# HGRN2 heads of a two-layer hybrid: urgent level steps, z from PSUM, output times z before the root factor, a second gate tile and a 32-byte tile

## Chip, cores and metric

The kernel runs on one core of a Trainium2 chip. The metric is the device time of one execution in microseconds, as a median over runs. The core's engines each work through their own instructions in order: TensorE (PE, with its weight loads shown as PEld), VectorE (DVE), ScalarE (ACT), GpSimd (POOL) and SyncE (SP, which here only issues DMAs).

## The reference

A stream of 1024 latent tokens and 256 context tokens, 1024 wide, goes through two layers. Layer 0 has neighbourhood-attention and mLSTM heads, layer 1 has 16 HGRN2 heads, which the change concerns. The arithmetic is fp32. Of layer 1, cut to the core:

```python
q, f_fwd, f_bwd, i, z = split(h @ w_in)                  # 2048 columns each, 16 heads of 128
f = lb + (1 - lb) * sigmoid(f_pre)                        # per direction
rec = silu(q), i, ((1 - f, log f) forward, (1 - f, log f) backward)
# per head and direction, S starts from the context's final state:
#   S_t = diag(f_t) S_(t-1) + (1 - f_t) i_t^T ;   o_t = S_t^T silu(q_t)
o = o_forward + o_backward
y = (rms(o, h_norm) * silu(z)) @ w_out
x = x + gate * y
```

## The kernel before, in words

The kernel is written in a tile framework. The order in which the program issues operations gives each a priority; the framework's scheduler keeps, with modelled times, the order of each engine by those priorities and by what is ready, and the engines then follow that order. `filler` adds 1000000 to the priority number of what it encloses, so that it comes last among what is ready. Tiles belong to pools; a tile name with n buffers waits for the buffer used n allocations before. Pools open from the left end of the core's SBUF, or, with `side="right"`, from its right end. PSUM has two banks each of "mm" (projection sums) and "tr" (transposes); while the heads run, three of "s" and one of "acc".

The large fp32 products are written in three parts, each with the fp32r type: `dense` (L125 to L131) multiplies high part by high part (L128), and the two mixed ones (L129, L130). They are called products in the text. Layer 0 and its output projection take the first 1880 us, the HGRN2 heads 1880 to 3350 us, the last output projection the rest.

The heads go one after another (the loop over `h` in `build`). For each:

- `hg_proj` (L882) makes the gates F (two directions, 1024 tokens) and Fc (256 context tokens) and q of the head, by products with 256 or 512 columns. Its weight slabs come from pool "w1" at the right. F and Fc are single tiles in a pool of their own (`self.fp`).
- `hg_intra` (L968) makes K = 1 - F, Q = q F (L979), and 32 small matmuls, the "strips" (`strip`, L995 to L997), for the diagonal blocks; then seven `hg_level` calls (L1016). Level l combines neighbouring blocks of 2^l tokens: ACT copies the chosen half of K into ksel (L1024), 32 strips multiply it with the chosen half of Q into a PSUM bank, DVE merges the result into D (`copy_predicated`, L1042), multiplies the other halves of K and Q in place by the block totals T (L1050), and makes the totals of the doubled blocks in a new tile gT0 to gT6 (L1052). At level 0, T is F itself. Strips of a level need Q and ksel of the level before.
- `hg_vz` (L912) makes v and z, by products of 256 columns with weights wzh and wzl in pool "hg" at the left. Of z's PSUM bank ACT makes a sigmoid (L933) and a copy (L934), and POOL multiplies the two (L935).
- `hg_close` transposes K; `hg_ctx` makes the context states; `hg_scan` (L1055) runs the recurrence over eight chunks and makes the outputs, in two halves of four chunks. A half stands in the only "acc" bank (L1073 to L1075): ACT squares and sums it (L1089), POOL makes the root factor ss (L154, L156), and DVE multiplies output, ss and z for each chunk (L1093), into z's tile.
- `hg_out` (L1128) transposes that z on TensorE (L1133), ACT scales it and POOL issues its DMA. It comes after `hg_proj` of the next head.
- `wo_sums` (L1103) and `y_diff` (L1119) prepare the last projection on POOL: four loads, four subtractions and four stores per call, one call in heads 0 to 7, two in heads 8 to 11.

So TensorE's stream of a head mixes products, strips, scan matmuls and transposes, and what stands between two strip groups is set by the scheduler.

Of the kernel before, what the change touches and what calls it, by code (L numbers as in the profile page):

```python
# [9 lines left out]
F32 = mybir.dt.float32  # L10
# [3 lines left out]
ALU = mybir.AluOpType  # L14
# [4 lines left out]
P = 128  # L19
D = 1024  # L20
KD = D // P
LAT = 1024
CTX = 256
SQ = 256
T = LAT + CTX
# [19 lines left out]
class Prog:  # L45
# [285 lines left out]
    @contextmanager  # L331
    def filler(self):
        p = self.tc.cur_priority
        self.tc.cur_priority = p + 1000000
        yield
        self.tc.cur_priority = p

# [544 lines left out]
    def hg_proj(self, h, pool, w=None):  # L882
        nc, a = self.nc, self.a
        st = {}
        col = lambda i: a["wc"][:, i * 2048 + h * P : i * 2048 + (h + 1) * P]
        lb, olb = self.lb[:, 0, h : h + 1], self.lb[:, 1, h : h + 1]
        F = self.t(self.fp, [P, 2, LAT], F32, "gF", 1)
        Fc = self.t(self.fp, [P, 2, CTX], F32, "gFc", 1)
        todo = [(d, t0, n) for d in range(2) for t0, n in ((LAT, CTX), (512, 512), (0, 512))]
        if w:  # L890

            todo.sort(key=lambda x: x[1] == 0)
        w = w or [None, None]
        for d, t0, n in todo:
            w[d] = w[d] or self.wring([col(1 + d)], P)
            ps = self.ps("mm", [P, n])
            self.proj_tr(ps, w[d], 0, t0, n)
            dst = Fc[:, d, :] if t0 == LAT else F[:, d, t0 : t0 + 512]
            nc.scalar.activation(dst, ps, AF.Sigmoid)
            nc.vector.tensor_scalar(out=dst, in0=dst, scalar1=olb, scalar2=lb, op0=ALU.mult, op1=ALU.add)  # L900
        q = {}
        w = self.wring([col(0)], P)
        for t0 in (512, 0):
            ps = self.ps("mm", [P, 512])
            self.proj_tr(ps, w, 0, t0, 512)
            q[t0 // 512] = self.t(pool, [P, 512], F32, "gq", 2)
            sg = self.t(pool, [P, 512], F32, "gsg", 1)
            nc.scalar.activation(sg, ps, AF.Sigmoid)
            nc.vector.tensor_tensor(out=q[t0 // 512], in0=sg, in1=ps, op=ALU.mult)
        return dict(F=F, Fc=Fc, q=q)  # L910

    def hg_vz(self, h, st, pool):  # L912
        nc, a = self.nc, self.a
        col = lambda i: a["wc"][:, i * 2048 + h * P : i * 2048 + (h + 1) * P]
        w = self.wblock(pool, "wz", [col(3), col(4)], KD, 256)
        v = self.t(pool, [P, NT, P], F32, "gv", 2)
        z = self.t(pool, [P, NT - 2, P], F32, "gz", 1)
        ps = self.ps("mm", [P, CTX])
        self.proj_tr(ps, w, 0, LAT, CTX)
        vT = self.t(pool, [P, CTX], F32, "gEc", 1)  # L920
        nc.scalar.copy(vT, ps)
        pt = self.ps("tr", [P, 2, P])
        for j in range(2):
            nc.tensor.transpose(pt[:, j, :], vT[:, j * P : (j + 1) * P], self.ident)
        nc.scalar.copy(v[:, 8:10, :], pt)
        for tt in range(0, 8, 2):

            ps = self.ps("mm", [P, 2, 256])
            for j in range(2):
                self.proj_nat(ps[:, j, :], w, tt + j, 0, 256)  # L930
            nc.scalar.copy(v[:, tt : tt + 2, :], ps[:, :, 0:P])
            sg = self.t(pool, [P, 2, P], F32, "gsg", 1)
            nc.scalar.activation(sg, ps[:, :, P:256], AF.Sigmoid)  # L933
            nc.scalar.copy(z[:, tt : tt + 2, :], ps[:, :, P:256])  # L934
            nc.gpsimd.tensor_tensor(out=z[:, tt : tt + 2, :], in0=z[:, tt : tt + 2, :], in1=sg, op=ALU.mult)  # L935
        st["v"], st["z"] = v, z


# [29 lines left out]
    def hg_intra(self, st, pool):  # L968
        nc = self.nc
        F, q = st["F"], st["q"]  # L970
        K = self.t(pool, [P, 2, LAT], F32, "gK", 1)
        nc.vector.tensor_scalar(out=K, in0=F, scalar1=-1.0, scalar2=1.0, op0=ALU.mult, op1=ALU.add)
        Q = self.t(pool, [P, 2, LAT], F32, "gQ", 1)
        ks = [self.t(pool, [P, 512], F32, "gkn", 4) for _ in range(2)]
        for hf in (1, 0):
            s = slice(hf * 512, (hf + 1) * 512)
            nc.vector.tensor_tensor(out=ks[hf], in0=K[:, 0, s], in1=K[:, 1, s], op=ALU.add)
            for d in range(2):
                nc.vector.tensor_tensor(out=Q[:, 1 - d, s], in0=q[hf], in1=F[:, d, s], op=ALU.mult)  # L979
        hv = dict(Q=Q, K=K, T=F, D=self.t(pool, [P, 8, 64], F32, "gD", 1))  # L980
        hv["A"] = self.t(pool, [P, 8, P], F32, "gA", 1)
        pa = self.ps("s", [P, 8, 64])
        for c in range(8):
            for b in range(2):
                o = c % 4 * P + b * 64
                self.strip(pa[:, c, :], b, ks[c // 4][:, o : o + 64], q[c // 4][:, o : o + 64])
        nc.vector.tensor_tensor(
            out=hv["D"], in0=pa, in1=self.lmask[:, 0, :].unsqueeze(1).to_broadcast([P, 8, 64]), op=ALU.mult
        )
        for lev in range(7):  # L990
            self.hg_level(hv, lev, pool)
        return hv
# [23 lines left out]
    def hg_level(self, H, lev, pool):  # L1016
        nc = self.nc
        n, h = LAT, 1 << lev
        nb = n // (2 * h)
        K, Q, A, D, Tt = H["K"], H["Q"], H["A"], H["D"], H["T"]  # L1020

        pick = lambda t: _skew(t[:, 0, :].rearrange("p (b s i) -> p b s i", s=2, i=h), 2, n)
        ksel = self.t(pool, [P, n], F32, "gksel", 1)
        nc.scalar.copy(ksel.rearrange("p (b s i) -> p b s i", s=2, i=h), pick(K))  # L1024
        pa = self.ps("s", [P, 8, 64])
        for c in range(8):
            for b in range(2):
                o = c * P + b * 64
                out = pa[:, c, :]
                if lev < 6:  # L1030
                    out = out.rearrange("p (b s i) -> p b s i", s=2, i=h)
                    rhs = pick(Q)[:, o // (2 * h) : (o + 64) // (2 * h)]
                else:
                    rhs = Q[:, 1 - b, c * P + (1 - b) * 64 : c * P + (2 - b) * 64]
                self.strip(out, b, ksel[:, o : o + 64], rhs)
        for b in range(2):
            s, e = slice(b * 64, (b + 1) * 64), slice((1 - b) * 64, (2 - b) * 64)
            if lev == 6:
                nc.scalar.copy(A[s, :, s], D[s])
                nc.scalar.copy(A[s, :, e], pa[s])  # L1040
        if lev < 6:
            nc.vector.copy_predicated(D, self.lmask[:, lev + 1, :].unsqueeze(1).to_broadcast([P, 8, 64]), pa)  # L1042
        Tv = Tt.rearrange("p d (b s) -> p d b s", s=2)


        m = 2 * nb
        for t, o, step in ((K, 1, m - 1), (Q, m + 1, -m - 1)):
            v = bass.AP(t.tensor, t.offset, [list(t.ap[0]), [n + h, 2], [2 * h, nb], [1, h]])
            tot = bass.AP(Tt.tensor, Tt.offset + o, [list(Tt.ap[0]), [step, 2], [2, nb], [0, h]])
            nc.vector.tensor_tensor(out=v, in0=v, in1=tot, op=ALU.mult)  # L1050
        Tn = self.t(pool, [P, 2, nb], F32, f"gT{lev}", 1)
        nc.vector.tensor_tensor(out=Tn, in0=Tv[:, :, :, 0], in1=Tv[:, :, :, 1], op=ALU.mult)  # L1052
        H["T"] = Tn

    def hg_scan(self, st, H, S, pool):  # L1055
        nc = self.nc
        v, z = st["v"], st["z"]
        Sf, Sb = S
        sb = {7: Sb}
        for c in range(7, 0, -1):  # L1060
            u = self.ps("s", [P, P])
            nc.tensor.matmul(u, lhsT=H["kn"][c // 4][1][:, c % 4, :], rhs=v[:, c, :], start=True, stop=True)
            s = self.t(pool, [P, P], F32, "gS1", 10)
            nc.vector.scalar_tensor_tensor(
                out=s, in0=sb[c], scalar=H["T"][:, 1, c : c + 1], in1=u, op0=ALU.mult, op1=ALU.add
            )
            sb[c - 1] = s
        for c in range(8):
            cs = slice(c * P, (c + 1) * P)
            if c % 4 == 0:  # L1070
                o4 = self.ps("acc", [P, 4, P])
            o = o4[:, c % 4, :]
# [3 lines left out]
            if c < 7:  # L1076
                u = self.ps("s", [P, P])
                nc.tensor.matmul(u, lhsT=H["kn"][c // 4][0][:, c % 4, :], rhs=v[:, c, :], start=True, stop=True)
                s = self.t(pool, [P, P], F32, "gS0", 2)
                nc.vector.scalar_tensor_tensor(  # L1080
                    out=s, in0=Sf, scalar=H["T"][:, 0, c : c + 1], in1=u, op0=ALU.mult, op1=ALU.add
# [4 lines left out]
            ss = self.t(pool, [P, 4], F32, "gss", 2)  # L1086
# [2 lines left out]
                nc.scalar.activation(jk, o4[:, i, :], AF.Square, accum_out=ss[:, i : i + 1])  # L1089
            self.rsqrt(ss, ss, 1.0 / P)  # L1090

            for i in range(c - 3, c + 1):
                nc.vector.scalar_tensor_tensor(  # L1093
                    out=z[:, i, :], in0=o4[:, i % 4, :], scalar=ss[:, i % 4 : i % 4 + 1], in1=z[:, i, :],
                    op0=ALU.mult, op1=ALU.mult,
                )

    def quarters(self, pool):
        two = [self.t(pool, [P, 2 * SQ], F32, t, 1) for t in ("gknc", "gEc")]
# [39 lines left out]
    def build(self):  # L1139
        tc, nc, a = self.tc, self.nc, self.a  # L1140
        dma = nc.sync.dma_start
        with ExitStack() as es:
# [22 lines left out]
            def load(name, shape, eng=nc.gpsimd):  # L1165
# [12 lines left out]
                out=self.qkn, in0=qkn[:, 0:1], scalar1=qkn[:, 1:2], scalar2=0.125, op0=ALU.mult, op1=ALU.mult  # L1178
# [22 lines left out]
            )  # L1201


            right = ExitStack()
            es.enter_context(right)
            self.open_h(right)
# [397 lines left out]
```

## Time and profile before

| | us |
|---|---|
| median of 3 runs | 3482.99 |
| lowest and highest run | 3482.43, 3485.25 |
| profiled execution, its own time | 3489.74 |
| span of the profile | 3488.0 |
| granted TensorE clock (1 is full) | 0.993 |
| busy: PE, DVE, ACT, POOL | 3409.5, 2098.0, 1478.0, 707.3 |

The span is what the profile covers; the run's own time is 1.7 us longer. A row of the timeline shows start, duration, engine, line, operation, output tile <- input tiles, output shape, input shape, and how many alike instructions are taken together (x32); the bracket has the idle time before it and what ended that. `gz`, `gq`, `gK` and so on are the tiles of the code; a product's row, mm<-wzh,hh, has the stationary and moving operands in no fixed order.

### The profile page before, as it was taken

The numbers are of one execution on the slowest core, as the hardware profiler recorded it, in microseconds if no ns is written. First come the engines' busy times: TensorE is split into PE (matmuls) and PEld (weight loads), VectorE is DVE, ScalarE is ACT, GpSimd is POOL, SyncE is SP. The second block draws the span as 40 slices with busy tenths as digits, with TensorE's granted clock in tenths as the row PEclk, the third lists the DMA queues.
The fourth block names the chain that finished last, engine by engine and source line by source line (L and its number), as shares of the span: only waits on it lengthen the run. The fifth ranks groups of instructions, "written<-read, shape, count | busy, mean of one in ns | idle before, by whom it ended". The sixth has DMA issues, their size and how long they took to land.

```text
span 3488.0 us, 64893 instructions
## 1 busy us (share of the span) xinstructions
PE 3409.5 (98%) x25100; PEld 2990.6 (86%) x25100; DVE 2098.0 (60%) x4855; ACT 1478.0 (42%) x3433; POOL 707.3 (20%) x1076
## 2 busy tenths in 40 slices
PE   8999999999999999999999999999999999999997
PEld 5679998889989888898888988988888888888876
DVE  4546665666655566777666555555555555555667
ACT  5445554554543444454354333333333333333442
POOL 2222221222111112221100112222223222100023
PEclk9999999999999999999999999999999999999999
DMA  5542222322233434444752111111112111110274
GB/s 202 175 130 61 79 77 76 91 78 75 79 89 99 145 117 127 132 129 143 218 162 70 46 58 55 58 59 58 57 57 67 61 58 49 49 37 31 85 233 151
DMA packets 331540, 333.60 MB, mean 96 GB/s; under 512 B 30984, under 2 KB 277960, under 8 KB 331232
## 3 DMA queue, kind: packets, MB, share of 16 engines
q1 hardware_dynamic: 291008, 222.76, 22.0%
q0 software_dynamic: 40224, 106.69, 9.0%
q8 instruction: 198, 3.24, 0.4%
q14 instruction: 110, 0.90, 0.1%
HBM read 259.40 MB, written 69.79 MB: 94 GB/s over the span
## 4 chain that ended last, share of the span: by engine, by line
PE 85%; DMA 4%; issue 3%; DVE 3%; POOL 2%; ACT 1%; SPq 0%; POOLq 0%; DVEq 0%; ACTq 0%
PE mm L128 18%; PE mm L129 18%; PE mm L130 18%; PE s L997 4%; PE acc L775 2%; PE mm L837 2%; PE mm L835 2%; PE mm L836 2%; PE tr L755 2%; PE acc L547 2%; PE s L556 2%; PE acc L537 1%; PE tr L1009 1%; PE acc L1073 1%; PE acc L1074 1%
## 5 line engine op out<-in xcount | busy, mean ns | idle before, releaser
L128 PE MATMUL mm<-hh,wh 128*128 128x512 f32 (+1 forms) x1600 | 584.5, 365 | 0.0
L129 PE MATMUL mm<-hl,wh 128*128 128x512 f32 (+1 forms) x1600 | 584.3, 365 | 0.0
L130 PE MATMUL mm<-hh,wl 128*128 128x512 f32 (+1 forms) x1600 | 583.5, 365 | 0.0
L128 PE MATMUL mm<-wh,hh 128*128 128x256 f32 (+1 forms) x1520 | 471.2, 310 | 1.7 <-ACT ev L317 0.6
L129 PE MATMUL mm<-wl,hh 128*128 128x256 f32 (+1 forms) x1520 | 469.9, 309 | 0.0
L130 PE MATMUL mm<-wh,hl 128*128 128x256 f32 (+1 forms) x1520 | 468.9, 309 | 0.3 <-DVE hl L262 0.3
L130 PEld LDWEIGHTS mm<-hh,wl 128*128 128x128 f32 x1600 | 301.3, 188 | 45.6 <-issue 0.6
L129 PEld LDWEIGHTS mm<-hl,wh 128*128 128x128 f32 x1600 | 301.6, 188 | 43.8 <-issue 0.2
L128 PEld LDWEIGHTS mm<-hh,wh 128*128 128x128 f32 x1600 | 301.6, 188 | 43.0 <-issue 0.2
L128 PEld LDWEIGHTS mm<-wh,hh 128*128 128x128 f32 x1520 | 286.5, 189 | 16.5 <-issue 0.9
L129 PEld LDWEIGHTS mm<-wl,hh 128*128 128x128 f32 x1520 | 286.5, 188 | 14.7 <-issue 2.9
L130 PEld LDWEIGHTS mm<-wh,hl 128*128 128x128 f32 x1520 | 286.4, 188 | 13.8 <-issue 1.5
L128 PE MATMUL mm<-wzh,hh 128*128 128x256 f32 x1024 | 292.8, 286 | 0.6 <-ACT gz L934 0.6
L129 PE MATMUL mm<-wzl,hh 128*128 128x256 f32 x1024 | 292.8, 286 | 0.0
L130 PE MATMUL mm<-wzh,hl 128*128 128x256 f32 x1024 | 291.5, 285 | 0.0
L73 DVE TENSOR_TENSOR wl<-wraw,wh 128x512 fp32r<-128x512 f32 x240 | 165.5, 694 | 129.2 <-ACT wh L72 121.5
L72 ACT CAST wh<-wraw 128x512 fp32r<-128x512 f32 x240 | 147.2, 618 | 198.9 <-PE mm L129 140.7
L1024 ACT COPY gksel<-gK 128x1024 f32<-128x1024 f32 x112 | 128.0, 1143 | 213.0 <-PE s L997 139.2
L128 PEld LDWEIGHTS mm<-wzh,hh 128*128 128x128 f32 x1024 | 193.5, 189 | 3.8 <-ACT gz L934 1.6
L129 PEld LDWEIGHTS mm<-wzl,hh 128*128 128x128 f32 x1024 | 193.4, 189 | 1.0
L130 PEld LDWEIGHTS mm<-wzh,hl 128*128 128x128 f32 x1024 | 193.3, 189 | 1.0
L835 PE MATMUL mm<-woh,yh 128*128 128x512 f32 x422 | 170.4, 404 | 9.8 <-DVE og L1366 5.2
(390 smaller groups left out, 7623.4 us busy)
## 6 DMA issues: line engine op xcount, KB each, us to landing
wraw<-in_wab_dram SPq DMA_DIRECT2D x112, 256.0 KB
wraw<-in_wc_dram SPq DMA_DIRECT2D x96, 256.0 KB
wraw<-yd SPq DMA_DIRECT2D x94, 256.0 KB
adar<-in_wada_dram POOLq DMA_DIRECT2D x32, 512.0 KB, 4.5
wraw<-in_wc_dram SPq DMA_DIRECT2D x128, 128.0 KB
md<-ev POOLq DMA_DIRECT2D x60, 256.0 KB, 2.8
mloz<-md SPq DMA_DIRECT2D x40, 256.0 KB
adar<-in_wada_dram SPq DMA_DIRECT2D x16, 512.0 KB
```

Of the source, the lines that this page charges most:

```text
L72: nc.scalar.copy(hi, x)
L73: nc.vector.tensor_tensor(out=lo, in0=x, in1=hi.bitcast(F32), op=ALU.subtract)
L128: mm(ps, lhsT=lh(k), rhs=rh(k), start=(start and k == 0), stop=False)
L129: mm(ps, lhsT=lh(k), rhs=rl(k), start=False, stop=False)
L130: m = mm(ps, lhsT=ll(k), rhs=rh(k), start=False, stop=(stop and k == nk - 1))
L547: nc.tensor.matmul(num, lhsT=qc[:, j, :], rhs=C[d][:, j, :], start=False, stop=(j == 1))
L556: nc.tensor.matmul(u, lhsT=st["k"][c][:, j * P : (j + 1) * P], rhs=vw, start=True, stop=True)
L755: nc.tensor.transpose(pt[:nk, i, :], pr[:, o : o + nk], self.ident)
L775: m = nc.tensor.matmul(yp[h64], lhsT=v[:, h64], rhs=pTs[hd][:nk, i, :], start=(i == turn[0]), stop=(i == turn[-1]), tile_position=(0, hd * ...
L835: mm(ps, lhsT=yh[k], rhs=w.h(kk), start=(kk == 0), stop=False)
L997: self.nc.tensor.matmul(out[s], lhsT=lhsT, rhs=rhs, start=True, stop=True, tile_position=(0, b * 64))
L1024: nc.scalar.copy(ksel.rearrange("p (b s i) -> p b s i", s=2, i=h), pick(K))
```

## The change

It has six parts.

1. A new context, `urgent`, subtracts 1000000 from the priority number. It stands around the strips of the diagonal blocks, and in a level around the ksel copy, the strips, and the steps of Q, K and T. The merge into D is not in it.
2. T of the next level is written in place over T's own tile (F), level by level; only the last one goes to a tile of its own. The last level takes its stationary operand from K itself, with no ksel copy.
3. F and Fc of odd heads come from pool "hg", those of even heads from the pool they had.
4. z times its sigmoid is one DVE operation from PSUM; the copy on ACT and the product on POOL go.
5. A half of the outputs is multiplied by z on DVE in one operation over four chunks, without the root; POOL then multiplies it by the root factors, which are broadcast along 128 columns.
6. A tile of 32 bytes per partition is opened at the right end of SBUF ahead of everything else there, and zeroed once.

```diff
@@ -332,6 +332,14 @@
     def filler(self):
         p = self.tc.cur_priority
         self.tc.cur_priority = p + 1000000
+        yield
+        self.tc.cur_priority = p
+
+
+    @contextmanager
+    def urgent(self):
+        p = self.tc.cur_priority
+        self.tc.cur_priority = p - 1000000
         yield
         self.tc.cur_priority = p
 
@@ -884,8 +892,9 @@
         st = {}
         col = lambda i: a["wc"][:, i * 2048 + h * P : i * 2048 + (h + 1) * P]
         lb, olb = self.lb[:, 0, h : h + 1], self.lb[:, 1, h : h + 1]
-        F = self.t(self.fp, [P, 2, LAT], F32, "gF", 1)
-        Fc = self.t(self.fp, [P, 2, CTX], F32, "gFc", 1)
+        fp = pool if h % 2 else self.fp
+        F = self.t(fp, [P, 2, LAT], F32, "gF", 1)
+        Fc = self.t(fp, [P, 2, CTX], F32, "gFc", 1)
         todo = [(d, t0, n) for d in range(2) for t0, n in ((LAT, CTX), (512, 512), (0, 512))]
         if w:
 
@@ -931,8 +940,7 @@
             nc.scalar.copy(v[:, tt : tt + 2, :], ps[:, :, 0:P])
             sg = self.t(pool, [P, 2, P], F32, "gsg", 1)
             nc.scalar.activation(sg, ps[:, :, P:256], AF.Sigmoid)
-            nc.scalar.copy(z[:, tt : tt + 2, :], ps[:, :, P:256])
-            nc.gpsimd.tensor_tensor(out=z[:, tt : tt + 2, :], in0=z[:, tt : tt + 2, :], in1=sg, op=ALU.mult)
+            nc.vector.tensor_tensor(out=z[:, tt : tt + 2, :], in0=sg, in1=ps[:, :, P:256], op=ALU.mult)
         st["v"], st["z"] = v, z
 
 
@@ -980,10 +988,11 @@
         hv = dict(Q=Q, K=K, T=F, D=self.t(pool, [P, 8, 64], F32, "gD", 1))
         hv["A"] = self.t(pool, [P, 8, P], F32, "gA", 1)
         pa = self.ps("s", [P, 8, 64])
-        for c in range(8):
-            for b in range(2):
-                o = c % 4 * P + b * 64
-                self.strip(pa[:, c, :], b, ks[c // 4][:, o : o + 64], q[c // 4][:, o : o + 64])
+        with self.urgent():
+            for c in range(8):
+                for b in range(2):
+                    o = c % 4 * P + b * 64
+                    self.strip(pa[:, c, :], b, ks[c // 4][:, o : o + 64], q[c // 4][:, o : o + 64])
         nc.vector.tensor_tensor(
             out=hv["D"], in0=pa, in1=self.lmask[:, 0, :].unsqueeze(1).to_broadcast([P, 8, 64]), op=ALU.mult
         )
@@ -1020,37 +1029,37 @@
         K, Q, A, D, Tt = H["K"], H["Q"], H["A"], H["D"], H["T"]
 
         pick = lambda t: _skew(t[:, 0, :].rearrange("p (b s i) -> p b s i", s=2, i=h), 2, n)
-        ksel = self.t(pool, [P, n], F32, "gksel", 1)
-        nc.scalar.copy(ksel.rearrange("p (b s i) -> p b s i", s=2, i=h), pick(K))
-        pa = self.ps("s", [P, 8, 64])
-        for c in range(8):
-            for b in range(2):
-                o = c * P + b * 64
-                out = pa[:, c, :]
-                if lev < 6:
-                    out = out.rearrange("p (b s i) -> p b s i", s=2, i=h)
-                    rhs = pick(Q)[:, o // (2 * h) : (o + 64) // (2 * h)]
-                else:
-                    rhs = Q[:, 1 - b, c * P + (1 - b) * 64 : c * P + (2 - b) * 64]
-                self.strip(out, b, ksel[:, o : o + 64], rhs)
+        out = self.ps("s", [P, 8, 64])
+        with self.urgent():
+            if lev < 6:
+                ksel = self.t(pool, [P, n], F32, "gksel", 1)
+                nc.scalar.copy(ksel.rearrange("p (b s i) -> p b s i", s=2, i=h), pick(K))
+            for c in range(8):
+                for b in range(2):
+                    o = c * P + b * 64
+                    r = out[:, c, :]
+                    if lev < 6:
+                        r = r.rearrange("p (b s i) -> p b s i", s=2, i=h)
+                        lhsT, rhs = ksel[:, o : o + 64], pick(Q)[:, o // (2 * h) : (o + 64) // (2 * h)]
+                    else:
+                        lhsT = K[:, b, o : o + 64]
+                        rhs = Q[:, 1 - b, c * P + (1 - b) * 64 : c * P + (2 - b) * 64]
+                    self.strip(r, b, lhsT, rhs)
+            for t, o, step in ((Q, n + 1, -n - 1), (K, 1, n - 1)):
+                v = bass.AP(t.tensor, t.offset, [list(t.ap[0]), [n + h, 2], [2 * h, nb], [1, h]])
+                tot = bass.AP(Tt.tensor, Tt.offset + o, [list(Tt.ap[0]), [step, 2], [2, nb], [0, h]])
+                nc.vector.tensor_tensor(out=v, in0=v, in1=tot, op=ALU.mult)
+            Tv = Tt[:, :, 0 : 2 * nb].rearrange("p d (b s) -> p d b s", s=2)
+            if lev == 6:
+                H["T"] = self.t(pool, [P, 2, nb], F32, "gT", 1)
+            nc.vector.tensor_tensor(out=H["T"][:, :, 0:nb], in0=Tv[:, :, :, 0], in1=Tv[:, :, :, 1], op=ALU.mult)
+        if lev < 6:
+            nc.vector.copy_predicated(D, self.lmask[:, lev + 1, :].unsqueeze(1).to_broadcast([P, 8, 64]), out)
+            return
         for b in range(2):
             s, e = slice(b * 64, (b + 1) * 64), slice((1 - b) * 64, (2 - b) * 64)
-            if lev == 6:
-                nc.scalar.copy(A[s, :, s], D[s])
-                nc.scalar.copy(A[s, :, e], pa[s])
-        if lev < 6:
-            nc.vector.copy_predicated(D, self.lmask[:, lev + 1, :].unsqueeze(1).to_broadcast([P, 8, 64]), pa)
-        Tv = Tt.rearrange("p d (b s) -> p d b s", s=2)
-
-
-        m = 2 * nb
-        for t, o, step in ((K, 1, m - 1), (Q, m + 1, -m - 1)):
-            v = bass.AP(t.tensor, t.offset, [list(t.ap[0]), [n + h, 2], [2 * h, nb], [1, h]])
-            tot = bass.AP(Tt.tensor, Tt.offset + o, [list(Tt.ap[0]), [step, 2], [2, nb], [0, h]])
-            nc.vector.tensor_tensor(out=v, in0=v, in1=tot, op=ALU.mult)
-        Tn = self.t(pool, [P, 2, nb], F32, f"gT{lev}", 1)
-        nc.vector.tensor_tensor(out=Tn, in0=Tv[:, :, :, 0], in1=Tv[:, :, :, 1], op=ALU.mult)
-        H["T"] = Tn
+            nc.scalar.copy(A[s, :, s], D[s])
+            nc.scalar.copy(A[s, :, e], out[s])
 
     def hg_scan(self, st, H, S, pool):
         nc = self.nc
@@ -1089,11 +1098,9 @@
                 nc.scalar.activation(jk, o4[:, i, :], AF.Square, accum_out=ss[:, i : i + 1])
             self.rsqrt(ss, ss, 1.0 / P)
 
-            for i in range(c - 3, c + 1):
-                nc.vector.scalar_tensor_tensor(
-                    out=z[:, i, :], in0=o4[:, i % 4, :], scalar=ss[:, i % 4 : i % 4 + 1], in1=z[:, i, :],
-                    op0=ALU.mult, op1=ALU.mult,
-                )
+            z4 = z[:, c - 3 : c + 1, :]
+            nc.vector.tensor_tensor(out=z4, in0=o4, in1=z4, op=ALU.mult)
+            nc.gpsimd.tensor_tensor(out=z4, in0=z4, in1=ss.unsqueeze(2).to_broadcast([P, 4, P]), op=ALU.mult)
 
     def quarters(self, pool):
         two = [self.t(pool, [P, 2 * SQ], F32, t, 1) for t in ("gknc", "gEc")]
@@ -1201,6 +1208,8 @@
             )
 
 
+            edge = es.enter_context(tc.tile_pool(name="edge", bufs=1, side="right"))
+            nc.vector.memset(self.t(edge, [P, 8], F32, "edge"), 0.0)
             right = ExitStack()
             es.enter_context(right)
             self.open_h(right)
```

Of the scheduled order: TensorE has the same 21160 matmuls, ACT 2730 instructions instead of 2806, POOL 921 instead of 953, DVE 4767 instead of 4703. All tiles at the right lie 32 bytes lower.

## Prediction

> **What bounds the kernel now.** The first view is the head of the page: the span, the busy share of each engine, and the chain that ended last.
>
> ```profile
> span 3488.0 us, 64893 instructions
> PE 3409.5 (98%) x25100; PEld 2990.6 (86%) x25100; DVE 2098.0 (60%) x4855; ACT 1478.0 (42%) x3433; POOL 707.3 (20%) x1076
> PE 85%; DMA 4%; issue 3%; DVE 3%; POOL 2%; ACT 1%; SPq 0%; POOLq 0%; DVEq 0%; ACTq 0%
> ```
>
> TensorE is busy for 98% and carries 85% of the chain. The HGRN2 heads fill the stretch from 1880 to 3350 us, so the second view is the windows (us of the stretch, then busy us and instructions of PE, PEld, DVE, ACT, POOL, the clock, the DMA share, GB/s), and the third is what TensorE waited for there (total us, times, longest).
>
> ```profile
> 1880.00:3350.00 1470.00, 1441.33 (x12526) 1299.13 (x12525) 834.08 (x1367) 526.30 (x1094) 276.51 (x383) 0.99 0.19 58
> ```
> ```profile
> PE s L997 <- DVE gQ L1050: 14.4, 10, 1.5
> PE tr L1133 <- DVE gz L1093: 6.3, 4, 1.9
> ```
>
> Of 1470 us only 28.7 are free of TensorE, and two waits are most of them: strips of level 1 wait for Q after level 0 (ten times, 1.4 each), and the z transposes wait four times for the normed z. DVE is busy for 57% and POOL for 19%, so work taken from them, or from ACT, gains nothing by itself. Time can move in three ways: stalls of TensorE, the way its instructions are mixed, and the time per product. The matmuls themselves stay: the compiled order of both kernels has 21160.
>
> The fourth view is the timeline of a steady head, from the last scan output (call its end T = 2172.96) to the strips of level 1.
>
> ```profile
> 2172.57 0.39 PE L1075 MATMUL acc<-gS,gQ 128*128 128x128 f32 x2
> 2173.00 2.50 DVE L979 TENSOR_TENSOR gQ<-gq,gF 128x512 f32<-128x512 f32 x4 [2.42 <-PE acc L1075]
> ...
> 2174.43 0.19 ACT L1089 ACTIVATION_READ_ACCUMULATOR gjk<-acc 128x1 f32 x1
> ...
> 2175.03 1.37 POOL L156 TENSOR_TENSOR gss<-gss,mhalf 128x4 f32<-128x4 f32 x1
> ...
> 2175.64 1.56 PE L997 MATMUL s<-gQ,gksel 128*64 128x64 f32 x32
> ...
> 2178.09 1.21 DVE L1050 TENSOR_TENSOR gQ<-gQ,gF 128x1024 f32<-128x1024 f32 x1
> ...
> 2179.45 0.76 PE L997 MATMUL s<-gQ,gksel 128*64 128x64 f32 x18 [1.45 <-DVE gQ L1050]
> ```
>
> After T the squares end at T+1.66 and the root at T+3.44; level 0's strips run, then the transposes, and TensorE stands still for 1.45 until T+6.49; with the strips' slow start (1.56 against 1.08 in the chain's rows below) about 2.0 us are lost in a head.
>
> The fifth view is the chain, by the first strips of heads 3, 4, 9, 13 and 14.
>
> ```profile
> 2165.24 1.08 PE s L997 x32
> ...
> 2254.20 1.08 PE s L997 x32
> ...
> 2698.88 1.11 PE s L997 x32
> ...
> 3069.31 1.08 PE s L997 x32
> ...
> 3160.14 1.08 PE s L997 x32
> ```
>
> A steady head takes 88.96. Four from 2698.88 take 370.43, which is 14.6 more than 4 x 88.96; head 13 takes 90.83, 1.9 more. The reasons of the 14.6 are in the timeline there:
>
> ```profile
> 2789.88 0.73 POOL L1110 TENSOR_TENSOR gEc<-gEc 128x256 f32<-128x256 f32 x1
> 2790.55 0.59 POOL L1116 DMA_DIRECT2D sw<-gEc  x1
> 2791.17 1.03 POOL L156 TENSOR_TENSOR gss<-gss,mhalf 128x4 f32<-128x4 f32 x1
> ...
> 2792.73 0.81 PE L1133 MATMUL tr<-ident,gz 128*128 128x128 f32 x3 [1.87 <-DVE gz L1093]
> ```
> ```profile
> 2710.39 1.04 PE L997 MATMUL s<-gQ,gksel 128*64 128x64 f32 x18
> ...
> 2713.77 0.44 PE L924 MATMUL tr<-ident,gEc 128*128 128x128 f32 x2
> ```
>
> The root stands behind a subtraction and a DMA issue of the weight sums on POOL, and a group of 32 strips is cut by four single transposes: 3.38 us from 2710.39 to 2713.77, where 1.1 of strips and 0.8 of transposes (the 0.81 above) would do: 1.4 lost, 0.35 per cut.
>
> **The change part by part.**
>
> *Strips, K, Q and T urgent.* In the compiled order no strip group is cut any more; the changes from strips to a transpose fall from 54 to 15. Cuts of heads 9 to 12 are counted in the 14.6 above; the others (heads 1 and 15, six cuts at 0.35) give **-2 us**. A transpose that sat alone among products cost nothing worth counting:
>
> ```profile
> 2166.72 0.28 PE L129 MATMUL mm<-wzl,hh 128*128 128x256 f32 x1
> ...
> 2167.30 0.28 PE L130 MATMUL mm<-wzh,hl 128*128 128x256 f32 x1
> ```
>
> Between these starts lie four product steps and one transpose: 0.58, less four steps of 0.117 (below) leaves 0.11 for the transpose. Bounds: -8 (0.1 for each of 88 fewer changes of kind) to 0.
>
> *Output times z at once, root factor on POOL.* Before, the acc bank came free after root and four DVE products; now after one. But z's transposes wait for a longer chain: squares T+1.66, root T+3.1 to 3.4, then one POOL product. The nearest rows for it are a group half as wide (busy us, mean ns, idle before) and one as wide (least, median and most ns):
>
> ```profile
> L935 POOL TENSOR_TENSOR gz<-gz,gsg 128x256 f32<-128x256 f32 x64 | 62.8, 982 | 166.0 <-ACT gz L934 165.5
> ```
> ```profile
> L1124 POOL TENSOR_TENSOR gknc<-gknc,gEc x8: 1264/1424/1897, 2069.3 to 2701.4; 128x512 f32<-128x512 f32 x8
> ```
>
> I take the median 1.42 of the one as wide (ends 0.98 and 1.90): z is ready at T+5.0 with handovers. In the new order of heads 4 to 8 TensorE has 13 products (1.5 us) and the strips (1.15 with their handover) behind T, then waits from T+2.65 to T+5.0: **2.35 idle**, against 2.0 now. Q for level 1 comes at the same time: four gQ to T+2.5, the z product and one more DVE operation to T+3.7, Q's 1.3 to T+5.0, so the same wait covers it. By this count over the new order: heads 4 to 8 lose 0.3 each (+1.5); heads 1, 2, 11 and 12 have some 5 us of products there and wait for nothing; heads 3 and 13 have 3 to 5 and wait about 0.7; head 14 has 1.1 and waits 2.6; head 10 1.0; head 9, where transposes of both halves follow the outputs with little or nothing between, about 8 (an estimate from the same chain, twice, with POOL's weight sums in it); head 15 is taken as now. Lost now: nine steady heads (2 to 8, 13, 14) at 2.0, 14.6 in 9 to 12, 1.9 in 13: 34.5; this is more than the idle share of these heads, since slow starts and cuts count as busy. Lost then: 5 x 2.35 + 2 x 0.7 + 2.6 + 1 + 8 = 24.8. So **-10 us**. Bounds: with each of 32 halves 0.97 later (rival C) it becomes +21; with the product at 0.98 (seven heads, 0.44 each) and head 9 covered, -21.
>
> *z from PSUM on DVE; levels without T tiles.* ACT and POOL lose work that waits for nothing (62.8 us of POOL). DVE gets 64 products, and T's steps now stand between levels. The rows of a level:
>
> ```profile
> L1050 DVE TENSOR_TENSOR gK<-gK,gT 128x1024 f32<-128x1024 f32 x96 | 123.7, 1289 | 0.0
> L1050 DVE TENSOR_TENSOR gQ<-gQ,gT 128x1024 f32<-128x1024 f32 x96 | 116.0, 1209 | 15.5 <-PE s L997 15.5
> L1042 DVE COPY_PREDICATED gD<-glm,s 128x512 f32<-128x512 uint8 x96 | 71.3, 743 | 93.0 <-PE s L997 93.0
> L909 DVE TENSOR_TENSOR gq<-gsg,mm 128x512 f32<-128x512 f32 x32 | 21.8, 682 | 5.0 <-ACT gsg L908 5.0
> ```
>
> In 31 gaps of the new order only 31 products stand between strip groups (3.7 us, 4.85 from group to group with the strips). DVE must fit 1.29 + 1.21 + 0.74, a T of 0.2 to 0.6, a z product (half of 0.68, say 0.4) and often a weight split (0.7): 4.3 to 4.9. That just fits, and Q needs only the first 1.3 of the gap, so a lag of 2.4 is covered: **0**. Uncovered, every 0.1 costs 3 us (rival B).
>
> *Second F tile*: **0**. It lets F of the next head be written while T is still updated in place in this one's; no row shows TensorE waiting for F now.
>
> *32-byte tile at the right.* It is written once (nothing), but moves every tile that opens from the right by 32 bytes. By the compiled addresses, before it a right tile and a left one stand 32 bytes apart within 64, after it not: 2544 products of 512 columns and 7279 of 256 come into the class in which stationary and moving operand agree. Spacing of unbroken products, by first and last start, 512 apart in class, 512 agreeing, 256 apart, 256 agreeing:
>
> ```profile
> 1183.95 0.39 PE L129 MATMUL mm<-wl,hh 128*128 128x512 f32 x1
> ...
> 1191.40 0.40 PE L128 MATMUL mm<-wh,hh 128*128 128x512 f32 x1
> ```
> ```profile
> 1676.50 0.40 PE L835 MATMUL mm<-woh,yh 128*128 128x512 f32 x1
> ...
> 1732.05 0.39 PE L837 MATMUL mm<-woh,yl 128*128 128x512 f32 x1
> ```
> ```profile
> 2447.60 0.28 PE L129 MATMUL mm<-wzl,hh 128*128 128x256 f32 x1
> ...
> 2452.50 0.28 PE L129 MATMUL mm<-wzl,hh 128*128 128x256 f32 x1
> ```
> ```profile
> 2016.50 0.28 PE L128 MATMUL mm<-hh,wh 128*128 128x256 f32 x1
> ...
> 2019.25 0.28 PE L130 MATMUL mm<-hh,wl 128*128 128x256 f32 x1
> ```
>
> 512 columns: 32 steps of 233 ns apart in class, 245 of 226.7 agreeing. 256 columns: 42 of 116.7 apart, 23 of 119.6 agreeing. If the class does this, 2544 x -6.3 = -16 and 7279 x about 2 = +14: **-2 us**, bounds -16 (the 256 rows differ for another reason) and +14 (the 512 rows do). The Trainium skill, "TensorE: Matmul & The Clock Gate", section "Back-to-back issue gap", gives a step by the column count alone; by that this term is 0 and the sum 2 us higher. The trace disagrees so far: 233 and 226.7 at one count.
>
> *End stage*: a few loads change order, nothing is taken off: 0, bounds ±4.
>
> **Sum:** -2 - 10 + 0 - 2 = -14 from the profiled execution's 3489.74 (span 3488.0 and 1.7 around it). That execution is 6.75 above the median of the runs, so on their scale 3482.99 - 14 = **3469 us**.
>
> **The rivals.** About 0.2% (7 us) can be told from no change: faster is under 3476, slower over 3490.
>
> A, the forecast: 3469, own range 3460 to 3479. Chance 0.42.
>
> B, DVE does not keep up with the levels: the 31 tight gaps grow by 0.4 each, +12: 3481. For it: 4.9 against 4.85 at the upper end. Against: 57% busy, and the cover of 2.4. Chance 0.20.
>
> C, slower: POOL's product becomes what the transposes wait for, in both halves of all 16 heads. For it: the root took 1.37 beside gQ and 1.03 in head 10, and the like product 1.26 to 1.90, so beside DVE's products it may come 0.34 + 0.63 = 0.97 later: 32 x 0.97 = +31: 3500. It decides from 0.66 per half (21 / 32). Against: some halves have cover. The Trainium skill, "SBUF — State Buffer", section "🔬 SBUF: two separate sides", says that GpSimd and a VectorE operation with two SBUF inputs lock each other out of a shared port pair; by that rule the product waits out a gQ or Q's 1.2. The 1.37 beside gQ agrees. Chance 0.25.
>
> D, 256-column products do not lose by the shift: 14 less, 3455. For it: runs of the two 256 rows differ in which operand is stationary, too. Chance 0.13.
>
> **How the numbers follow.** Likeliest is A, 3469. The range goes from 3446 (D and 9 more from stalls) to 3501 (C at its price); about 0.12 lies above and 0.04 below. Faster: 0.36 of A and D, 0.49. Same: B less a little, and 0.06 of A, 0.26. Slower: C, 0.25.
>
> **What would show it.** The steady head's period of 88.96 would hold within 0.5, and the four from head 9 fall by 6 or more; the z transposes would wait for a POOL gz, 2.3 in heads 4 to 8 and about 8 in head 9, with the POOL product at 1.3 to 1.9. Group to group of tight levels would be 4.85; more is B. Layer 0's 512-column steps would be 227, the wz steps 119 (117 is D). C shows as z waits of a microsecond more in both halves. If the period changes while no wait shows, the mix or step time was misjudged.

## The result, and the profile after

The changed kernel takes 3468.68 us (median of 8 runs, 3466.75 to 3475.56) beside 3482.74 of the kernel before (8 runs, 3481.58 to 3485.26). The ratio is 0.9962, 95% interval 0.9951 to 0.9973: 14 us less. 3469 was forecast, also 14 less. The number is right; the experiments show that two of its terms are wrong and make up for each other, and that TensorE's stalls stand elsewhere than it put them.

The head of the page after, then the windows of the heads and of what lies behind them, in the columns of before:

```profile
span 3468.4 us, 64675 instructions
PE 3386.4 (98%) x25100; PEld 2983.5 (86%) x25100; DVE 2089.2 (60%) x4824; ACT 1440.2 (42%) x3353; POOL 674.2 (19%) x1044
PE 86%; DMA 4%; DVE 3%; issue 3%; ACT 1%; POOL 1%; SPq 0%; POOLq 0%; DVEq 0%; ACTq 0%
```
```profile
1880.00:3330.00 1450.00, 1414.66 (x12508) 1279.95 (x12506) 819.07 (x1328) 483.87 (x1008) 242.85 (x351) 1.00 0.19 58
3330.00:3468.00 138.00, 115.58 (x456) 90.44 (x454) 104.41 (x129) 44.55 (x77) 54.36 (x45) 0.90 0.64 202
```

TensorE's busy time fell by 23 us with the same number of matmuls, but its idle share in the heads did not fall: 1450.00 - 1414.66 = 35.3 us are free of it now, 28.7 were. So the gain is not in the stalls as a whole. What TensorE waited for, in the whole kernel:

```profile
PE tr L1140 <- POOL gz L1103: 8.9, 8, 4.5
PE s L1006 <- DVE gQ L1051: 8.8, 11, 4.0
PE s L1006 <- DVE gQ L987: 8.6, 7, 1.6
```

L987 makes Q for level 0 (L979 before), L1051 is a level's step. The waits for the steps fell from 14.4 to 8.8, those of the z transposes grew from 6.3 to 8.9, and those for Q of level 0 from 1.7, the row of before below, to 8.6.

```profile
PE s L997 <- DVE gQ L979: 1.7, 1, 1.7
```

A steady head (head 6, T = 2427.18 now):

```profile
2426.79 0.39 PE L1084 MATMUL acc<-gS,gQ 128*128 128x128 f32 x2
...
2427.22 2.50 DVE L987 TENSOR_TENSOR gQ<-gq,gF 128x512 f32<-128x512 f32 x4 [2.58 <-PE acc L1084]
...
2429.24 1.44 POOL L156 TENSOR_TENSOR gss<-gss,mhalf 128x4 f32<-128x4 f32 x1
...
2429.86 1.56 PE L1006 MATMUL s<-gQ,gksel 128*64 128x64 f32 x32 [1.15 <-DVE gQ L987]
...
2430.76 1.04 POOL L1103 TENSOR_TENSOR gz<-gz,gss 128x512 f32<-128x512 f32 x1
...
2431.86 0.66 PE L1140 MATMUL tr<-ident,gz 128*128 128x128 f32 x4 [0.43 <-POOL gz L1103]
...
2433.03 1.18 PE L1006 MATMUL s<-gQ,gksel 128*64 128x64 f32 x32 [0.30 <-DVE gQ L1051]
```

Level 0's strips start at T+2.68, the transposes at T+4.68 and the strips of level 1 at T+5.85. TensorE stands for 1.9 us here, in three places: 1.15 for Q of level 0, 0.43 for POOL's product, 0.30 for Q of level 1. Heads start at these rows (first strips of heads 6, 7, 9 and 13):

```profile
2418.71 1.15 PE L1006 MATMUL s<-gq,gkn 128*64 128x64 f32 x32
...
2507.63 1.15 PE L1006 MATMUL s<-gq,gkn 128*64 128x64 f32 x32
...
2685.47 1.15 PE L1006 MATMUL s<-gq,gkn 128*64 128x64 f32 x32
...
3043.84 1.15 PE L1006 MATMUL s<-gq,gkn 128*64 128x64 f32 x32
```

A steady head takes 88.92 (88.96 before), and heads 9 to 12 take 358.4 (370.4). The step of two products changed too: 32 steps of 512 columns and, in the heads, 74 of 256 columns with wz:

```profile
1179.80 0.40 PE L129 MATMUL mm<-wl,hh 128*128 128x512 f32 x1
...
1187.10 0.39 PE L128 MATMUL mm<-wh,hh 128*128 128x512 f32 x1
```
```profile
2167.28 0.28 PE L129 MATMUL mm<-wzl,hh 128*128 128x256 f32 x1
...
2175.67 0.28 PE L128 MATMUL mm<-wzh,hh 128*128 128x256 f32 x1
```

512 columns: 7.30 / 32 = 228 ns where 233 stood. wz: 8.39 / 74 = 113.4 ns where 116.7 stood, and where the prediction put 119.

### The profile page after: what moved, and what is told of

It reads as the page before. It is cut to its first block, busy times and chain, and to the rows that moved or that the text cites. A ratio compares the mean times of both kernels' runs of the same rounds, so it can differ in the third digit from the quotient of the medians.

```text
span 3468.4 us, 64675 instructions
## 1 busy us (share of the span) xinstructions
PE 3386.4 (98%) x25100; PEld 2983.5 (86%) x25100; DVE 2089.2 (60%) x4824; ACT 1440.2 (42%) x3353; POOL 674.2 (19%) x1044
## 4 chain that ended last, share of the span: by engine, by line
PE 86%; DMA 4%; DVE 3%; issue 3%; ACT 1%; POOL 1%; SPq 0%; POOLq 0%; DVEq 0%; ACTq 0%
PE mm L128 19%; PE mm L129 19%; PE mm L130 19%; PE s L1006 4%; PE acc L783 2%; PE tr L763 2%; PE mm L843 2%; PE mm L844 2%; PE mm L845 2%; PE acc L555 2%; PE s L564 2%; PE acc L545 1%; PE acc L1082 1%; PE acc L1083 1%; PE acc L1084 1%
## 5 line engine op out<-in xcount | busy, mean ns | idle before, releaser
L128 PEld LDWEIGHTS mm<-wh,hh 128*128 128x128 f32 x1520 | 289.8, 191 | 14.6 <-issue 1.1
L1036 ACT COPY gksel<-gK 128x1024 f32<-128x1024 f32 x96 | 110.8, 1154 | 223.9 <-PE s L1006 113.7
L1051 DVE TENSOR_TENSOR gQ<-gQ,gF 128x1024 f32<-128x1024 f32 x112 | 139.3, 1244 | 90.4 <-PE s L1006 89.9
```

The costliest lines, as they stand in the source:

```text
L128: mm(ps, lhsT=lh(k), rhs=rh(k), start=(start and k == 0), stop=False)
```

## The experiments

Two theories stood at the start. **O** (the prediction): the order of the heads is worth 12, the 32-byte tile 2. **S**: the step of two products hangs on where the operands lie modulo 256 bytes, and most of the gain is that. Every ratio below is to the kernel before, run beside it; 0.001 is 3.5 us. Kernel n is the kernel of experiment n. "Layer 0" ends at the first strips of head 0, "the heads" at the last z transpose; both are read from one profiled execution. One reading of layer 0 tells little under 4 us: in the ten kernels that have the 32-byte tile and not the swap of experiments 9 and 12, it takes 1890.3 to 1894.5.

**1. The tile alone** (e1), on the kernel before:

```diff
+            edge = es.enter_context(tc.tile_pool(name="edge", bufs=1, side="right"))
+            nc.vector.memset(self.t(edge, [P, 8], F32, "edge"), 0.0)
```

> The kernel before with the 32-byte tile alone. Theory O (order): the tile is worth -2 and the order of the heads -12, so 3481. Theory S (spacing): the step of two products depends on how far stationary and moving operand lie apart modulo 256 bytes, not 64. From the steps of both traces (512 columns 233 apart and 227.5 agreeing, about 2060 of them; 256 columns 118.4 apart and 119.4 agreeing in layer 0, about 3500; wz then at 0 against 192, seen in neither) the tile alone gives -11 + 4 + 2 = -5, 3478, with layer 0 shorter by 5 to 8 and wz at 117.

Measured: ratio 0.9986 (0.9978 to 0.9995), -4.9. Layer 0 1898.3 to 1894.5, heads 1452.5 to 1450.0. That is S's number, though O's -2 is inside the interval and layer 0 fell by less than the 5 to 8 that S named.

**2. The change without the tile** (e2): the two lines above taken out of the changed kernel.

> The changed kernel without the 32-byte tile. Theory O: 2 us slower than the changed kernel, 3471. Theory S: 512-column steps go back to 233 (+11), 256-column ones of layer 0 to 118 (-5), and wz (at 128 against 224, seen in neither trace) from 114 to about 117 (+8): 3480 to 3483, that is nearly the time before; the reordering by itself is then worth about nothing.

Measured: ratio 1.0001 (0.9992 to 1.0010). The reordering without the tile is worth nothing that can be told; O's 3471 falls. The wz step here, wz at 128 and hh at 224 modulo 256:

```profile
2175.28 0.28 PE L129 MATMUL mm<-wzl,hh 128*128 128x256 f32 x1
...
2183.97 0.28 PE L128 MATMUL mm<-wzh,hh 128*128 128x256 f32 x1
```

8.69 / 74 = 117.4, against 113.4 for the same stretch with the tile, and the waits are the same to a tenth of a microsecond (tr for POOL gz 8.9, strips for gQ 8.8 and 8.6). On every engine the two traces have the same instructions in the same order, the tile's own memset apart. So the tile by itself makes the difference, 13.6 us by the two ratios with about 5 either way.

**3. Without urgent** (e3): `cur_priority = p - 1000000` became `cur_priority = p`.

> The changed kernel with urgent() doing nothing. Theory O: strip groups are cut by single transposes again at 0.35 a cut, and the level steps wait behind evictions on DVE: 5 to 10 slower than the changed kernel, 3474 to 3479. Theory S: within 3 of it, since the order moves stalls from some heads to others.

Measured: ratio 0.9972 (0.9961 to 0.9982) beside 0.9962 of the changed kernel: 3.5 slower, and the intervals overlap. Steady heads are shorter (87.9), head 14 (92.4 for 85.4) and heads 11 and 12 are longer, head 15 is shorter (102.5 for 106.9). Unclear in size; between the two expectations.

**4. The root product on DVE** (e4):

```diff
-            nc.gpsimd.tensor_tensor(out=z4, in0=z4, in1=ss.unsqueeze(2).to_broadcast([P, 4, P]), op=ALU.mult)
+            nc.vector.tensor_tensor(out=z4, in0=z4, in1=ss.unsqueeze(2).to_broadcast([P, 4, P]), op=ALU.mult)
```

> The changed kernel with the root product on DVE instead of POOL. If POOL's product is what the z transposes wait for (8.9 us of waits, 9.4 idle in head 9), heads 4 to 9 lose less: 5 to 10 faster than the changed kernel, 3459 to 3464. If Q of level 1 on DVE comes as late anyway, the steady heads stay as they are or lose 0.7 each, and only head 9 gains: 3463 to 3470.

Measured: ratio 0.9950 (0.9937 to 0.9962), some 4 faster than the changed kernel, with overlapping intervals. As in the second case expected, steady heads stay (89.0) and head 9 gains (88.2 for 95.5), but heads 10 and 11 give 7 of it back. So POOL's product is not what holds the steady heads.

**5 to 7. The place of wz, in one and the same order** (e5, e6, e7): kernel 1 with a pool of 128, 192 or 64 bytes opened ahead of pool "hg". All tiles of that pool move with wz.

```diff
+                pad = l1.enter_context(tc.tile_pool(name="pad", bufs=1))
+                nc.vector.memset(self.t(pad, [P, 32], F32, "pad"), 0.0)
                 pool = l1.enter_context(tc.tile_pool(name="hg", bufs=2))
```

(32 columns are 128 bytes; 48 and 16 in the other two.)

> The kernel before with the 32-byte tile at the right and 128 bytes ahead of pool hg at the left: wz lies at 128 modulo 256 and hh at 192, as in the changed kernel, and nothing of the order is changed. Theory S: the wz step goes from 117 to 114 and the heads lose another 3 x 3190 = 10 us: 3470 where the tile alone gave 3480, that is 13 to 16 under the kernel before; the whole gain of the change without its reordering. Theory O': the 114 comes from the new order (fewer evictions beside these products), and the time stays at 3480.

> As before with 192 bytes: wz and hh both at 192 modulo 256. Theory S: the wz step is that of agreeing 256-column operands, 119 to 120, and the heads are 6 to 9 us longer than with the tile alone: 3487 where that gave 3480. Theory O': 117, as with the tile alone.

> As before with 64 bytes: wz at 64, hh at 192. If what matters is whether the distance is 64, 117; if what matters is that both operands are not in the same 128 bytes or that the distance is below 256, 114 to 117. Seen in no trace so far; it only maps the step.

Runs of 42 steps, with wz at 128 (e5), then with wz at 192, where hh is (e6):

```profile
2438.40 0.28 PE L129 MATMUL mm<-wzl,hh 128*128 128x256 f32 x1
...
2443.17 0.28 PE L129 MATMUL mm<-wzl,hh 128*128 128x256 f32 x1
```
```profile
2534.45 0.28 PE L129 MATMUL mm<-wzl,hh 128*128 128x256 f32 x1
...
2539.47 0.28 PE L129 MATMUL mm<-wzl,hh 128*128 128x256 f32 x1
```

4.77 / 42 = 113.6 and 5.02 / 42 = 119.5. The places alone set the step, for on every engine these traces have the same instructions in the same order as kernel 1's, the pad's memset apart. The means over all steps of wz under 150 ns (from the traces), by the places of wz and hh modulo 256 (from the compiled addresses; in nine of ten products wz is the moving operand and hh the stationary one):

| wz, hh | kernel | mean ns | heads, us |
|---|---|---|---|
| 0, 224 | before | 117.1 | 1452.5 |
| 0, 192 | e1 | 116.2 | 1450.0 |
| 64, 192 | e7 | 118.6 | 1453.6 |
| 128, 192 | e5 | 114.9 | 1446.1 |
| 192, 192 | e6 | 119.5 | 1453.9 |
| 128, 192 | after | 115.0 | 1436.9 |
| 128, 224 | e2 | 118.3 | 1449.7 |

The time of e5 is 0.9982 (0.9973 to 0.9991), -6.3, and not the -13 to -16 expected. The step is as expected by its median (117 to 114), but the mean of e1 was 116.2 already, so 1.3 ns x 3200 = 4 us is what the heads could lose and did lose (1450.0 to 1446.1). So "the whole gain is spacing" falls as well: at the same addresses the changed order has 9 us less in the heads. e6 and e7 have one run each, 3485.88 and 3484.30 beside a median of 3484.30 of the kernel before; their heads are 3.9 and 3.6 longer than e1's, where the steps alone (+3.3 and +2.4 ns, 3200 times) would make 10 and 8: a steady head grew by 0.5 and 0.4, but in e6 heads 10, 11 and 13 became shorter, by 0.7, 0.7 and 1.2. So a sum over steps can be more than the heads gain or lose.

**8. Root product on DVE and no urgent** (e8): edits 3 and 4 together.

> The changed kernel with the root product on DVE and urgent() doing nothing. Without urgent steady heads took 87.9 instead of 88.9 but the others more; with the product on DVE head 9 took 88.2 instead of 95.5. If the two add, heads 4 to 8 gain 5 and head 9 7 over the changed kernel without urgent: 3462 to 3465, the fastest of all; if the scheduler only moves the stalls on, 3466 to 3472.

A miss: 1.0012 (1.0002 to 1.0021), 3488.86. The two do not add: it is 14 slower than kernel 3 and 22 slower than kernel 4 by the ratios. TensorE waits for z's root product on DVE (tr for DVE gz: 10.0 us in 12 waits) and for the acc bank (7.1 in 9).

**9. The weights of layer 0 at 128** (e9): kernel 4, with the two pools swapped.

```diff
-            mlk = l0.enter_context(tc.tile_pool(name="mlk", bufs=1))
             self.wp = l0.enter_context(tc.tile_pool(name="w0", bufs=2))
+            mlk = l0.enter_context(tc.tile_pool(name="mlk", bufs=1))
```

> The changed kernel with the root product on DVE, and pool w0 of layer 0 opened ahead of pool mlk, so that the weights of layer 0 lie at 128 modulo 256 beside hh at 192, as wz does in the heads; nothing of the order is meant to change. Theory S, by mean steps: 3840 products of 256 columns with w0 moving from 119.4 to 115 (-17), 576 the other way round from 119.4 to 117.5 (-1), 1872 of 512 columns from 228.5 to 231 to 233 (+5 to +8): 8 to 13 faster than the kernel with the root product on DVE alone, a ratio of 0.991 to 0.993 to the kernel before, all of it in layer 0. If the 115 belongs to wz for another reason than its place, layer 0's 256-column step stays at 119.4 or goes to 118 and the kernel gets slower or stays: 0.995 to 0.997.

Measured: 0.9906 (0.9889 to 0.9922), 3454.56; about 15 under kernel 4 by the ratios, 10.5 by the profiles: layer 0 is 12.0 shorter (1890.9 to 1878.9), and the heads, in the same order, 2.2 longer (1434.0 to 1436.2). The same 116 steps of 256 columns in the changed kernel and here:

```profile
237.67 0.28 PE L128 MATMUL mm<-wh,hh 128*128 128x256 f32 x1
...
251.59 0.28 PE L130 MATMUL mm<-wh,hl 128*128 128x256 f32 x1
```
```profile
238.16 0.28 PE L128 MATMUL mm<-wh,hh 128*128 128x256 f32 x1
...
251.32 0.28 PE L130 MATMUL mm<-wh,hl 128*128 128x256 f32 x1
```

13.92 / 116 = 120.0 and 13.16 / 116 = 113.4. The 113 to 115 belongs to the places, not to wz. The 512-column steps with w0 moving rose as S had it, from 229.7 to 233.1 in the mean.

**10. z as before** (e10), in the changed kernel:

```diff
-            nc.vector.tensor_tensor(out=z[:, tt : tt + 2, :], in0=sg, in1=ps[:, :, P:256], op=ALU.mult)
+            nc.scalar.copy(z[:, tt : tt + 2, :], ps[:, :, P:256])
+            nc.gpsimd.tensor_tensor(out=z[:, tt : tt + 2, :], in0=z[:, tt : tt + 2, :], in1=sg, op=ALU.mult)
```

> The changed kernel with z made as before (copy on ACT, product on POOL). The prediction held this part at 0: within 3 of the changed kernel, a ratio of 0.9955 to 0.997; POOL takes 63 us more, so the z transposes may wait a little longer. If DVE's 64 products were what the tight levels lack, it would be 3 to 10 faster.

Measured: 0.9907 (0.9892 to 0.9922), 3454.74: about 19 faster than the changed kernel by the ratios, more than any case expected. In the profile the heads have 1427.0 for 1436.9 and what follows them 133.2 for 141.2; head 9 has 87.2 for 95.5, head 15 100.6 for 106.9. The waits of the transposes for POOL are less, though POOL does more:

```profile
PE s L1007 <- DVE gQ L988: 8.8, 8, 2.7
PE s L1007 <- DVE gQ L1052: 7.8, 14, 2.0
...
PE tr L1141 <- POOL gz L1104: 3.1, 7, 0.4
```

Most of the 10 us of the heads are stalls: between the first strips and the last z transpose TensorE stands for 24.0 us, 33.1 in the changed kernel. The edit changes the scheduled order as well as DVE's load; which of the two takes the stalls off was not separated. What follows the heads is uncertain by some us: kernel 2, in the order of the changed kernel, has 137.5 there, and kernel 12, in the order of this one, 134.3.

**11. Root and z in four DVE operations, as before** (e11), in the changed kernel:

```diff
-            z4 = z[:, c - 3 : c + 1, :]
-            nc.vector.tensor_tensor(out=z4, in0=o4, in1=z4, op=ALU.mult)
-            nc.gpsimd.tensor_tensor(out=z4, in0=z4, in1=ss.unsqueeze(2).to_broadcast([P, 4, P]), op=ALU.mult)
+            for i in range(c - 3, c + 1):
+                nc.vector.scalar_tensor_tensor(
+                    out=z[:, i, :], in0=o4[:, i % 4, :], scalar=ss[:, i % 4 : i % 4 + 1], in1=z[:, i, :],
+                    op0=ALU.mult, op1=ALU.mult,
+                )
```

> The changed kernel with the outputs' root and z in four DVE operations a half, as before. The prediction put -10 on the shorter hold of the acc bank and the chain of the z transposes together. If the chain through POOL's product is what the change loses by, this is 3 to 6 faster than the changed kernel, 0.9945 to 0.9955; if the acc bank matters more, TensorE waits for acc in the first half of every head and it is 3 to 10 slower, 0.997 to 0.999.

Measured: 1.0080 (1.0065 to 1.0095), 3514.97: 41 slower than the changed kernel and 28 slower than the one before, four times what was expected at most. What TensorE waits for in its heads:

```profile
PE tr L1142 <- DVE gz L1102: 19.3, 6, 3.6
PE s L1006 <- DVE gQ L987: 19.1, 8, 2.7
PE mm L128 <- DVE gz L943: 10.3, 8, 2.0
```

The third wait is new: products wait for a bank whose z DVE has not yet read. The timeline of DVE there:

```profile
2260.33 1.36 POOL L156 TENSOR_TENSOR gss<-gss,mhalf 128x4 f32<-128x4 f32 x1
...
2261.73 1.13 DVE L1102 SCALAR_TENSOR_TENSOR gz<-acc,gss,gz 128x128 f32<-128x128 f32 x4 [0.59 <-POOL gss L156]
...
2262.77 1.22 DVE L1051 TENSOR_TENSOR gQ<-gQ,gF 128x1024 f32<-128x1024 f32 x1
...
2265.73 1.19 DVE L1055 TENSOR_TENSOR gF<-gF 128x1024 f32<-128x1024 f32 x1
2266.84 0.41 DVE L943 TENSOR_TENSOR gz<-gsg,mm 128x256 f32<-128x256 f32 x1
```

DVE stands for the root of POOL, and Q, T and z of the next products are queued behind that. So with z and T on DVE and without the early product of outputs and z the rest of the change loses to the kernel before. This edit, too, changes the scheduled order; what part of the 41 that makes was not separated.

**12. Both gains together** (e12): kernel 10 with the swap of 9.

> The two that gained, together: the changed kernel with z made as before (ACT copy, POOL product) and pool w0 opened ahead of pool mlk. If the order in the heads and the place of layer 0's weights are independent, the ratio to the kernel before is 0.9907 with another -11 to -12 of layer 0: 0.987 to 0.988, about 3443. If the order in the heads depends on addresses after all, or end stage and heads give some of it back, it is 0.990.

Measured: 0.9892 (0.9875 to 0.9908), 3446.69, the fastest of all and under both kernels. It lies between the two cases expected: 5 under kernel 10 by the ratios, with about 8 either way, where 11 to 12 was expected. Layer 0 is 8.8 shorter than in kernel 10 (1892.8 to 1884.0); heads and end keep nearly what they had (1427.3 for 1427.0, 134.3 for 133.2).

## Why the prediction was right, and where it was not

1. *What bounds the kernel.* Right: TensorE stays at 98%, and ACT's and POOL's savings show nowhere as time.

2. *Spacing, -2.* **This term failed, in the class of the wz products.** By places modulo 64 wz and hh would agree with the tile, and their 3200 steps would grow by about 2: +6 of the +14 for 256 columns. They shrank by 2.1 (117.1 to 115.0): -7. Places count modulo 256 at least, and wz moved from 0 to 128 with the tiles that the change adds to and takes from the pools at the left. The rest was right in kind: layer 0's 512-column steps fell from 232.6 to 229.0 in the mean (1880 steps under 300 ns, -7 us; the long runs from 233 to 228), its 256-column ones rose from 118.3 to 119.5 (3800 under 150 ns, +5). With about -1 from the few steps of 512 columns left over in the heads, the steps add up to -10 for the term. By time, kernel 5 has -6 with all places as in the changed kernel, with 3 either way. Rival D, "256 columns do not lose", was half of it: layer 0 loses, wz gains. The Trainium skill's rule in "TensorE: Matmul & The Clock Gate", section "Back-to-back issue gap", a step by the column count alone, does not hold here: 113.6 and 119.5 in kernels 5 and 6, at 256 columns and in the same order.

3. *Order, -2 and -10.* **This term failed too: it is too large,** by kernel 2 clear of the noise. At equal places (kernel 5) the changed kernel is 0.0020 lower by ratio: -7, with about 5 either way. Without the tile (kernel 2) it is 0, of which 1.2 ns x 3200 = +4 is wz's worse place: -4, with about 3 either way. So -4 to -7 in place of -12. The -10 also mixes two scales: the 14.6 lost in heads 9 to 12 is counted above four steady heads, which carry 2.0 each themselves, and the 24.8 from no loss at all. On the one scale it is 22.6 instead of 14.6 and the term -18, further off. By heads, against kernel 5: 4 to 8 lose 0.4 each (88.50 to 88.92; 0.3 was forecast); 9 to 12 gain 10.3 (368.7 to 358.4), where 14.6 less 9 = 5.6 was forecast and 13.6 is what one scale gives; and head 15, which was taken as it was, loses 4.2 (102.7 to 106.9). Its last z transposes alone stand for this long:

```profile
3326.54 0.66 PE L1140 MATMUL tr<-ident,gz 128*128 128x128 f32 x4 [4.53 <-POOL gz L1103]
```

What follows the heads has 4 us more (137.2 to 141.2) in this one profile; kernel 2, with the same order, has 137.5, so that is no part of the order.

4. *The chain of the transposes.* **Near in its length, wrong in what TensorE waits for.** In heads 4 to 8 a stall of 2.35 was forecast, all of it behind level 0's strips; 1.9 stands, and 1.15 of it ahead of them. The prediction let these strips run right behind the 13 products, from T+1.5, but they read Q, which its own count had ready at T+2.5. With the strips at T+2.68, POOL's product and Q of level 1 come only 0.43 and 0.30 late. So the sign that was named, z transposes waiting 2.3 in these heads, did not show. In all five of them:

```profile
PE s L1006 <- DVE gQ L987: 5.8, 5, 1.2
PE tr L1140 <- POOL gz L1103: 2.2, 5, 0.4
PE s L1006 <- DVE gQ L1051: 1.5, 5, 0.3
```

POOL's product took 1.07 in the mean, not the 1.42 of the like row:

```profile
L1103 POOL TENSOR_TENSOR gz<-gz,gss 128x512 f32<-128x512 f32 x32 | 34.2, 1070 | 2.4
```

Head 9 was to wait about 8 for the transposes of both halves; it stands for 9.4, but the transposes make 1.7 of that. Q of levels 0 and 1 makes 1.2 and 1.4, the acc bank 1.1, and Q of the next level 4.0, of which 1.06 is that DVE took 2.29 for it beside a difference on POOL, and 1.23 elsewhere:

```profile
2690.72 3.37 DVE L987 TENSOR_TENSOR gQ<-gq,gF 128x512 f32<-128x512 f32 x4 [0.99 <-PE acc L1084]
...
2690.91 1.42 POOL L1103 TENSOR_TENSOR gz<-gz,gss 128x512 f32<-128x512 f32 x1
...
2692.38 0.66 PE L1140 MATMUL tr<-ident,gz 128*128 128x128 f32 x4 [1.70 <-POOL gz L1103]
...
2699.61 2.12 POOL L1131 TENSOR_TENSOR gknc<-gknc,gEc 128x512 f32<-128x512 f32 x1 [1.43 <-DMA gEc<-yd]
2700.52 2.29 DVE L1051 TENSOR_TENSOR gQ<-gQ,gF 128x1024 f32<-128x1024 f32 x1
...
2702.96 1.34 PE L1006 MATMUL s<-gQ,gksel 128*64 128x64 f32 x20 [3.99 <-DVE gQ L1051]
```

5. *z on DVE at 0.* Wrong as a part: undone it gives 10 us in the heads and 19 in all (kernel 10). The rows of the level were right (a tight gap is 4.81 us from group to group, 4.85 forecast), so rival B, as it was put, did not happen. The forecast added the parts; kernels 8 and 11 show that they depend on each other.

6. *Rival C* did not happen: the transposes wait 8.9 us in eight places for POOL's product, where they waited 6.3 in four for DVE's; C wanted 31 more. Half of the 8.9 is the one wait in head 15 above. The second F tile was not tried by itself.

So -14 was met by -6 of spacing and -7 of order (by kernel 5) or -10 and -4 (by kernel 2), where -2 and -12 were forecast: the sum is right by two errors of opposite sign, and that it came within 1 us is luck.

## What to carry to other kernels

Where TensorE is busy for 98%, measure the step of back-to-back products by the places of both operands, in each pool, as a mean over all steps and not as a median: 5 ns in 119 over thousands of products is worth as much as a reordering, and swapping two pools can buy it. What a part of a change is worth hangs on the parts beside it: undoing one here cost 41 us, undoing another gained 19. In the first, DVE waited in order for a late factor, and all that was queued behind it was late too. A sum of parts that comes out right is no evidence for its terms; undo each by itself.

## What the runs showed of the hardware

- The step of 256-column products in parts of fp32r went from 113.4 to 120.0 ns, and that of 512-column ones from 227 to 233, by where the operands lie modulo 256 bytes: 256 columns are fastest with the moving operand at 128 and the stationary one at 192 and slowest where both are at 192; 512 columns are fastest where both agree (227 to 230 in the means; 232 to 233 with one at 192 and the other at 224, or the moving one at 128 and the stationary one at 192). The instructions had the same order in the kernels compared (before, 1, 5, 6 and 7; 4 and 9). Whether the distance or the places themselves count, and why, is not known; other places were not tried.
- A DVE and a POOL operation with two SBUF inputs each hold one another up: Q took 2.29 us beside POOL's difference, 1.23 in the level steps elsewhere, and ended 1.08 after POOL did; four gQ took 3.37 beside POOL's root product and 2.50 where none ran, and that product took 1.42 for 1.04. The Trainium skill, "SBUF — State Buffer", section "🔬 SBUF: two separate sides", says that GpSimd and a VectorE operation with two SBUF inputs lock each other out of a shared port pair for a whole instruction; these rows agree.
